# Weight-stationary products of a decoder layer: three matmuls of 256 columns in place of one of 512 and one of 256

## The chip, the cores and the metric

The kernel runs on one core of a Trainium2 chip. The metric is the device time of one execution in microseconds (us); before the change it is 1414.1 us, the median of three runs (1414.02 to 1414.1 us). All times below come from these runs or from one profiled execution of the same kernel.

## The reference

One decoder layer on 256 tokens of width 2048, batch 1, all in float32. Three sublayers follow each other, each as `h = layer_norm(2**0.25 * h + f(h))`:

```
h = x @ w_in                      # 2048 x 7216; q_a, k_a, v_a, q_b, six K/V groups, gates
y_a = sliding-window attention (16 heads, 2 K/V heads, sinks)
y_b = native sparse attention  (compressed + selected + window branches, 16 heads)
mix = (sigmoid(g_a) * (y_a @ w_branch_swa) + sigmoid(g_b) * (y_b @ w_branch_nsa)) @ w_mix_out
xa  = cross-attention of h with mem (256 rows), 4 heads of 128:  w_q, w_kv, w_o
ff  = square(relu(h @ mlp_w1)) @ mlp_w2      # 2048 x 8192 and 8192 x 2048
```

Nearly all of the work is matrix products of 256 rows with weights read once from HBM (268 MB).

## The kernel before

*High and low parts.* Every float32 operand of a large product is split in two: `h`, the value rounded to the narrower format that TensorE multiplies (`float32r`), and `l`, what is left. A product is then three: h·h, h·l and l·h. ScalarE writes `h` (line 198), VectorE subtracts it to get `l` (line 199).

*Chunks.* All weights of the layer go through one stream of chunks, mostly of 128 x 1024 numbers (512 KB), in the list `chunks`. `run_chunks` goes through the list. For a chunk it issues loads into one of five `raw` buffers, splits chunks ahead (up to three further than the chunk that TensorE works on, `AHEAD`), lets other jobs (attention, norms, transposes; the class `Side`) issue one step each, issues the chunk's matmuls, and after a block's last chunk empties the sums (`post`). A chunk index in `evac_first` has its sums emptied ahead of the last split. Nothing reorders the instructions later: each engine runs them as they were issued.

*Three kinds of products.* In `block_x` the inputs are stationary and the weights move, 512 columns at a time (lines 231 to 238). In `block_b` and `block_w` a 128 x 128 tile of weights is stationary and the inputs of all 256 rows move, so that the result comes out transposed. I call a tile with one slice of 128 rows of the weights, a k, a unit.

- `block_b` (lines 318, 319): the high weights meet the high and the low inputs, which lie side by side, in one matmul of 512 columns; the low weights meet the high inputs in one of 256. Each tile takes a whole PSUM bank, and the two halves of a bank are added afterwards by `halves` (ScalarE copies one, VectorE adds the other; lines 332 to 336). It does the four query blocks, the K and Q of the cross-attention and 14 blocks of 512 columns of the first MLP product.
- `block_w` with `mm_w` (lines 246 to 249): three matmuls of 256 columns into the same half of a bank, so that two tiles share one bank and the sums are complete. It does the first 1,024 columns of the MLP. Block c, the keys and values of the first projection, calls `mm_w` too, on other places of its chunk.

*Places of the weights.* A chunk's `shift` says where in its `h` and `l` buffers the split starts. Without a shift, h starts at byte 448 and l at byte 192 modulo 512, as in block c and `block_x`; `block_b` rotates through three shifts (h at 448, 320, 128; l at 192, 64, 384); `block_w` shifts by 16 and 112 numbers (h at 0, l at 128). The high and low inputs start at 448 throughout.

*Norms.* `norm_a` scales a piece on ScalarE (line 1037), multiplies by the gain on VectorE (1038) and adds the bias on GpSimd (1039) unless told otherwise. `finish` runs the last norm beside the last rows of the second MLP product.

The functions that are touched stand here with their lines:

Of the kernel before, what the change touches and what calls it, by code (L numbers as in the profile page):

```python
# [18 lines left out]
P = 128  # L19
# [19 lines left out]
def fp(ap):  # L39
    return ap.bitcast(F32)  # L40


class Chunk:
    def __init__(self, loads, n, mm, pre=None, with_split=None, post=None, cap=AHEAD, extra=None, parts=None, shift=(0, 0)):
        self.loads, self.n, self.mm = loads, n, mm
        self.pre, self.with_split, self.post, self.cap = pre, with_split, post, cap
        self.extra, self.shift = extra, shift
        self.parts = parts or [((lambda r: r[:, :n]),) * 2]


class Parts:
# [11 lines left out]

    def both(self, k):
        return self.tiles[k // 8][:, k % 8].rearrange("p i s -> p (i s)")
# [45 lines left out]
def layer(ctx: ExitStack, tc: tile.TileContext, x, mem, w_in, attn_sinks, rel_bias_table,  # L111
# [77 lines left out]
    def emit_splits(upto):  # L189
        while state["split"] <= min(upto, len(chunks) - 1):  # L190
# [15 lines left out]
    def run_chunks():  # L206
        for i, ch in enumerate(chunks):
# [4 lines left out]
            ahead = i + min(ch.cap, 1 if i < 3 else 2 if i < 6 else AHEAD)  # L212
# [92 lines left out]

    def block_b(w, n0, rhs, evac, tags=("acc",) * 4, pre=None):


        box = {}
        for k0 in range(0, KD, 2):  # L310
            def mm(h, l, k0=k0):
                if k0 == 0:
                    box["t"] = [bank(tag, "acc") for tag in tags]
                for a in range(2):
                    k = k0 + a
                    for t, o in enumerate(box["t"]):
                        c = slice((4 * a + t) * P, (4 * a + t + 1) * P)
                        nc.tensor.matmul(o, lhsT=h[:, c], rhs=rhs.both(k), start=k == 0, stop=False)  # L318
                        nc.tensor.matmul(o[:, :S], lhsT=l[:, c], rhs=rhs(k)[0], start=False, stop=k == KD - 1)  # L319

            def post():
                evac(box["t"])

            loads = [(lambda r: r[:, :1024].rearrange("p (a n) -> p a n", a=2),
                      w[k0 * P:(k0 + 2) * P, n0:n0 + 512].rearrange("(a p) n -> p a n", p=P))]
            chunks.append(Chunk(loads, 1024, mm, pre=pre if k0 == 0 else None, post=post if k0 + 2 == KD else None,
                                shift=((0, 96, 48)[len(chunks) % 3],) * 2))

    def halves(dst, t, scale=None):

        if scale is None:
            nc.scalar.copy(dst, t[:, S:])
            nc.vector.tensor_add(dst, t[:, :S], dst)
        else:
            nc.scalar.mul(dst, t[:, S:], scale)
            nc.vector.scalar_tensor_tensor(dst, t[:, :S], scale, dst, op0=OP.mult, op1=OP.add)
# [161 lines left out]

    def kv_parts(k):
        def pairs(v0, v1):  # L500
            return (lambda r: r[:, 128:896].rearrange("p (b v n) -> p v b n", v=2, n=P)[:, v0:v1],
                    lambda r: r[:, 128:896].rearrange("p (v b n) -> p v b n", v=2, n=P)[:, v0:v1])

        def cols(c0, c1):
            return (lambda r: r[:, c0:c1],) * 2
        if k == 0:
            return [pairs(1, 2), cols(896, 1072), pairs(0, 1), cols(0, 128)]
        return [pairs(0, 2), cols(896, 1072), cols(0, 128)]
# [62 lines left out]
    def make_c():  # L571
        for k in range(KD):
            def mm(h, l, k=k):
# [5 lines left out]
                first, last, V = k == 0, k == KD - 1, slice(640, 1072)  # L579
# [9 lines left out]
                else:  # L589
                    mm_x({(0, 0): a[0][:, :432], (1, 0): a[1][:, :432]},  # L590
                         lambda s: xh[:, rows[s]], lambda s: xl[:, rows[s]], h, l, [(640, 1072)], False, last)
# [770 lines left out]
```

## Time and profile before

| | |
|---|---|
| median of three runs | 1414.1 us |
| profiled execution | 1414.3 us, span 1412.3 us |
| TensorE matmuls | 1394.8 us busy, 99% of the span, 7,458 instructions |
| VectorE | 919.2 us, 65% |
| ScalarE | 721.7 us, 51% |
| GpSimd | 113.5 us, 8% |
| granted clock of TensorE | 0.997 of full speed on the mean |
| DMA | 190 GB/s on the mean |

Matmuls are pipelined: a row's duration runs from start to modelled end, and the next matmul starts before that end. How fast TensorE goes is read from the starts. An idle stretch of another engine is no loss while TensorE has work.

### The profile page before, as it was taken

How to read it: one execution, taken by the hardware profiler on the slowest of the kernel's cores; microseconds unless marked ns; L12 is line 12 of the kernel's file. 1: busy time of each engine (PE TensorE's matmuls, PEld its weight loads, DVE VectorE, ACT ScalarE, POOL GpSimd, SP SyncE). 2: the span in 40 equal slices, each digit the busy share in tenths (PEclk: the TensorE clock that was granted, in tenths of full speed). 3: DMA queues.
4: the chain of work that ended last, by engine and by line, in shares of the span. 5: the costliest groups of instructions: out<-in, count | busy, mean ns of one | idle time of the engine just before them, and what ended most of it. 6: DMA issues, size and time to landing. Idle time of an engine off the chain costs nothing.

```text
span 1412.3 us, 20010 instructions
## 1 busy us (share of the span) xinstructions
PE 1394.8 (99%) x7458; PEld 1196.6 (85%) x7458; DVE 919.2 (65%) x1501; ACT 721.7 (51%) x1177; POOL 113.5 (8%) x111
## 2 busy tenths in 40 slices
PE   9999999999999999999999999999999999999996
PEld 8988888888888888898898888888888888888885
DVE  5677887677764756766955656556565555755566
ACT  5566676665664444455454444444454444444452
POOL 1000221111110400220320000000000000000002
PEclk9999999999999999999999999999999999999998
DMA  8786655555557585574466666666676666576662
GB/s 267 230 258 181 186 168 164 165 153 161 149 150 252 175 297 184 174 243 139 139 186 194 186 189 190 184 190 180 194 240 195 195 193 193 179 208 193 194 193 89
DMA packets 108529, 268.43 MB, mean 190 GB/s; under 512 B 9920, under 2 KB 24832, under 8 KB 107664
## 3 DMA queue, kind: packets, MB, share of 16 engines
q1 hardware_dynamic: 106096, 256.49, 59.9%
q0 software_dynamic: 2048, 10.54, 2.2%
q8 instruction: 58, 0.95, 0.3%
q14 instruction: 39, 0.32, 0.1%
q10 hardware_dynamic: 288, 0.13, 0.1%
HBM read 264.97 MB, written 2.15 MB: 189 GB/s over the span
## 4 chain that ended last, share of the span: by engine, by line
PE 67%; issue 26%; DVE 5%; ACT 1%; POOL 0%; DMA 0%; DVEq 0%; SPq 0%; ACTq 0%; POOLq 0%
PE acc L238 22%; PE acc L318 20%; PE acc L319 10%; DVE l L199 2%; PE acc L248 1%; PE acc L249 1%; PE acc L246 1%; PE acc L231 1%; PE acc L233 1%; PE acc L232 1%; PE pt L749 1%; PE o L758 1%; PE lg L715 1%; PE lg L714 1%; PE hid L610 1%
## 5 line engine op out<-in xcount | busy, mean ns | idle before, releaser
L199 DVE TENSOR_TENSOR l<-raw,h 128x1024 fp32r<-128x1024 f32 (+4 forms) x501 | 585.9, 1178 | 381.6 <-ACT h L198 377.6
L198 ACT CAST h<-raw 128x1024 fp32r<-128x1024 f32 (+4 forms) x501 | 493.4, 994 | 441.6 <-PE acc L238 205.7
L318 PE MATMUL acc<-h2t,h 128*128 128x512 f32 x896 | 314.7, 395 | 0.0
L319 PE MATMUL acc<-h2t,l 128*128 128x256 f32 x896 | 251.7, 281 | 0.0
L318 PEld LDWEIGHTS acc<-h2t,h 128*128 128x128 f32 x896 | 168.4, 188 | 40.0
L319 PEld LDWEIGHTS acc<-h2t,l 128*128 128x128 f32 x896 | 168.6, 188 | 0.0
L238 PE MATMUL acc<-h,xt 128*128 128x512 f32 (+1 forms) x504 | 149.8, 394 | 0.0
L238 PE MATMUL acc<-l,ah 128*128 128x512 f32 x476 | 146.6, 389 | 0.0
L238 PE MATMUL acc<-h,ah 128*128 128x512 f32 x476 | 146.5, 389 | 0.0
L238 PE MATMUL acc<-h,al 128*128 128x512 f32 x476 | 146.5, 389 | 0.0
L238 PEld LDWEIGHTS acc<-l,ah 128*128 128x128 f32 x476 | 89.3, 188 | 18.6
L238 PEld LDWEIGHTS acc<-h,al 128*128 128x128 f32 x476 | 89.3, 188 | 18.6
L238 PEld LDWEIGHTS acc<-h,ah 128*128 128x128 f32 x476 | 89.3, 188 | 18.5
L238 PEld LDWEIGHTS acc<-h,xt 128*128 128x128 f32 x504 | 91.1, 188 | 14.8
L318 PE MATMUL acc<-xt,h 128*128 128x512 f32 x256 | 91.4, 397 | 0.0
L238 PE MATMUL acc<-l,xt 128*128 128x512 f32 (+1 forms) x252 | 79.6, 388 | 0.0
L319 PE MATMUL acc<-xt,l 128*128 128x256 f32 x256 | 71.9, 281 | 0.0
L238 PE MATMUL acc<-h,mt 128*128 128x512 f32 x224 | 63.2, 394 | 0.0
L745 POOL TENSOR_TENSOR p<-p,st 128x512 f32<-128x512 f32 x36 | 39.1, 1086 | 297.5 <-DVE st L740 135.2
L734 ACT ACTIVATE p<-p,st 128x256 f32<-128x256 f32 (+1 forms) x96 | 42.7, 447 | 36.4 <-DVE st L729 36.4
L318 PEld LDWEIGHTS acc<-xt,h 128*128 128x128 f32 x256 | 48.1, 188 | 10.9 <-ACT gt L550 0.3
L238 PE MATMUL acc<-h,yt 128*128 128x512 f32 x192 | 55.5, 395 | 0.0
(298 smaller groups left out, 2025.7 us busy)
## 6 DMA issues: line engine op xcount, KB each, us to landing
raw<-in_mlp_w_dram SPq DMA_DIRECT2D x256, 512.0 KB, 4.5
raw<-in_w_in_dram SPq DMA_DIRECT2D x96, 512.0 KB, 3.6
raw<-in_w_mix_out_dram SPq DMA_DIRECT2D x32, 512.0 KB, 4.7
raw<-in_w_branch_swa_dram SPq DMA_DIRECT2D x16, 512.0 KB, 3.7
raw<-in_w_branch_nsa_dram SPq DMA_DIRECT2D x16, 512.0 KB, 4.6
raw<-in_xa_w_kv_dram SPq DMA_DIRECT2D x16, 512.0 KB, 4.3
raw<-in_w_in_dram SPq DMA_DIRECT2D x16, 408.0 KB, 4.7
tbias<-udram POOLq DMA_DIRECT2D x8, 512.0 KB, 5.2
```

What stands on the lines that cost most here:

```text
L198: nc.scalar.copy(dst(h), src(raws[c]))
L199: nc.vector.tensor_sub(dst(l), src(raws[c]), fp(dst(h)))
L231: nc.tensor.matmul(a, lhsT=xh(s), rhs=h[:, c0:c1], start=first, stop=False)
L232: nc.tensor.matmul(a, lhsT=xh(s), rhs=l[:, c0:c1], start=False, stop=False)
L233: nc.tensor.matmul(a, lhsT=xl(s), rhs=h[:, c0:c1], start=False, stop=last)
L238: nc.tensor.matmul(acc[s, b], lhsT=lhs(s), rhs=rhs[:, c0:c1], start=False, stop=False)
L246: nc.tensor.matmul(a, lhsT=h[:, c], rhs=xh, start=first and (t % 2 == 0 if opens is None else t in opens), stop=False)
L248: nc.tensor.matmul(a, lhsT=h[:, c], rhs=xl, start=False, stop=False)
L318: nc.tensor.matmul(o, lhsT=h[:, c], rhs=rhs.both(k), start=k == 0, stop=False)
L319: nc.tensor.matmul(o[:, :S], lhsT=l[:, c], rhs=rhs(k)[0], start=False, stop=k == KD - 1)
L734: nc.scalar.activation(p[:, c:c + w], p[:, c:c + w], AF.Exp, bias=nm[:, i:i + 1], accum_out=sm[:, i:i + 1])
L745: nc.gpsimd.tensor_mul(pr, pr, sm.unsqueeze(2).to_broadcast([P, nr, 512 // nr]))
```

## The change

Every product with stationary weights becomes a `block_w`: `block_b` and `halves` are removed. 896 units of the MLP, 256 of the query blocks and 128 of the cross-attention change from a pair of matmuls to three. A bank then holds two complete tiles, which one copy (`copy_any`, ScalarE and VectorE in turn) empties; in the MLP ScalarE takes the relu of a bank and VectorE multiplies it by the bank itself. The MLP has eight blocks of 1,024 columns, alternately on the four `acc` banks and on the four others.

Block c's split is written in five pieces instead of three, so that its key weights begin at other places (h at 256, l at 128 modulo 512). The first two chunks of the cross-attention's K are split into two buffers of their own (`kspare`), and `boost` lets four chunks around there split one or two further ahead. `norm_a` adds the bias on VectorE now; one piece of the second norm stays on GpSimd. The last query block, in place of the first and third, has its sums emptied first.

```diff
-            for src, dst in ch.parts:
-                nc.scalar.copy(dst(h), src(raws[c]))
-                nc.vector.tensor_sub(dst(l), src(raws[c]), fp(dst(h)))
+            for src, dst, *low in ch.parts:
+                h_ap = dst(h)
+                nc.scalar.copy(h_ap, src(raws[c]))
+                nc.vector.tensor_sub((low or [dst])[0](l), src(raws[c]), fp(h_ap))
...
-            ahead = i + min(ch.cap, 1 if i < 3 else 2 if i < 6 else AHEAD)
+            ahead = i + ch.boost + min(ch.cap, 1 if i < 3 else 2 if i < 6 else AHEAD)
...
+    KEYS = (464, 496)
...
+        vals = [(lambda r: raw(r, 1, 2, 1), at(0, 2, True)), (lambda r: r[:, 896:1072], at(256, 176))]
+        ks = [(lambda r: r[:, 0:128], *keys(0, 128)), (lambda r: raw(r, 0, 3, 0), *keys(128, 3, True)),
+              (lambda r: raw(r, 0, 1, 1), *keys(512, 1, True))]
+        return vals + ks
...
-                mm_w(outs, xh, xl, h, l, first, last, (0, 1, 4), (2, 3, 4), (0, 128, 512, 256, 384))
+                mm_w(outs, xh, xl, h[:, KEYS[0]:], l[:, KEYS[1]:], first, last, (0, 1, 4), (2, 3, 4), (0, 128, 512, 256, 384))
...
-            halves(qraw[i][:, 4 * j + b, :], t)
+            copy_any(qraw[i][:, 4 * j + 2 * b:4 * j + 2 * b + 2, :], two(t))
...
-    block_b(w_in, COL_QA, xk, lambda tiles: evac_q(0, 0, tiles), tags=("lg", "pt", "acc", "acc"))
-    evac_first.add(len(chunks) - 1)
-    block_b(w_in, COL_QA + 512, xk, evac_qa)
+    block_w(w_in, COL_QA, 512, xk, lambda tiles: evac_q(0, 0, tiles), tags=("lg", "pt"))
+    block_w(w_in, COL_QA + 512, 512, xk, evac_qa)
...
-        (add or nc.gpsimd).tensor_add(v, v, gb[:, 1, c0:c0 + w])
+        (add or nc.vector).tensor_add(v, v, gb[:, 1, c0:c0 + w])
...
+    def kspare(j):
+        if j == 0:
+            box["kspare"] = box["pb"].tile([P, 4, 1024], F32R, tag="memraw", name="kspare")
+        return box["kspare"][:, 2 * j], box["kspare"][:, 2 * j + 1]
+
+    c0 = len(chunks)
+    block_w(xa_w_kv[0], 0, 512, me, evac_t("kt", None))
+    for j in range(2):
+        chunks[c0 + j].extra = lambda j=j: kspare(j)
+    for i, b in enumerate((1, 2, 2, 1)):
+        chunks[c0 - 2 + i].boost = b
...
-    block_b(xa_w_q[0], 0, hk, evac_t("qt", 128 ** -0.5), pre=lambda: side.require("ln1"))
+    block_w(xa_w_q[0], 0, 512, hk, evac_t("qt", 128 ** -0.5), pre=lambda: side.require("ln1"))
...
-                nc.gpsimd.tensor_mul(box["a"][k // KD][:, k % KD:k % KD + 2, :], two(r), two(r))
+                nc.vector.tensor_mul(box["a"][k // KD][:, k % KD:k % KD + 2, :], two(t), two(r))
...
-    block_w(mlp_w1[0], 0, 1024, hk, evac_a(0))
-    for f in range(2, 16):
-        block_b(mlp_w1[0], 512 * f, hk, evac_b(f), tags=("acc",) * 4 if f % 2 else alt)
+    for f in range(8):
+        block_w(mlp_w1[0], 1024 * f, 1024, hk, evac_a(f), tags=alt if f % 2 else ("acc",) * 4)
```

How the order of the instructions moves, at three places. On TensorE, in the first MLP product, the order before is pairs of a 512-column and a 256-column matmul (`h2t` are the transposed inputs, `h` and `l` the weights, `acc` the sums):

```order
L318 MATMUL acc<-h2t_6736,h 128x512
L319 MATMUL acc<-h2t_6736,l 128x256
L318 MATMUL acc<-h2t_6736,h 128x512
L319 MATMUL acc<-h2t_6736,l 128x256
L318 MATMUL acc<-h2t_6736,h 128x512
L319 MATMUL acc<-h2t_6736,l 128x256
```

and after the change it is threes of 256 columns at the same place:

```order
L245 MATMUL acc<-h2t_7130,h 128x256
L247 MATMUL acc<-h2t_7130,h 128x256
L248 MATMUL acc<-h2t_7130,l 128x256
L245 MATMUL acc<-h2t_7130,h 128x256
L247 MATMUL acc<-h2t_7130,h 128x256
L248 MATMUL acc<-h2t_7130,l 128x256
```

So a unit has one instruction more and the same 768 columns, and the low inputs meet the high weights in a matmul of their own.

On VectorE, where the mixer's last sums are emptied and the norm before the cross-attention begins, the order before has three splits of the K weights ahead of the sums (the last 3 of the 17; lines 1014 and 1020 are sums and statistics, 1038 the gain, `l` the low part of a split):

```order
L199 TENSOR_TENSOR l<-raw,h 128x1024 x17
L1014 SCALAR_TENSOR_TENSOR res<-res,acc 128x512 x4
L1020 BN_STATS stats<-res 128x6 x4
...
L1031 SCALAR_TENSOR_TENSOR rstd<-mv,rstd 128x1 x2
L1038 TENSOR_TENSOR res<-res,gb_5450 128x512
L199 TENSOR_TENSOR l<-raw,h 128x1024
L1038 TENSOR_TENSOR res<-res,gb_5450 128x512
L199 TENSOR_TENSOR l<-raw,h 128x1024 x3
```

and after the change five, two of them in `kspare`, with each gain (1011) followed by its bias (1012):

```order
L198 TENSOR_TENSOR l<-raw,h 128x1024 x14
L198 TENSOR_TENSOR kspare<-raw,kspare 128x1024 x2
L198 TENSOR_TENSOR l<-raw,h 128x1024 x3
L987 SCALAR_TENSOR_TENSOR res<-res,acc 128x512 x4
L993 BN_STATS stats<-res 128x6 x4
...
L1004 SCALAR_TENSOR_TENSOR rstd<-mv,rstd 128x1 x2
L1011 TENSOR_TENSOR res<-res,gb_5736 128x512
L1012 TENSOR_TENSOR res<-res,gb_5736 128x512
L198 TENSOR_TENSOR l<-raw,h 128x1024
```

Two splits moved ahead of the sums, and the bias came from GpSimd's queue into VectorE's.

On VectorE at the end of the kernel, the order before, from the first gain of the last norm to the sum of the last bank, is:

```order
L1038 TENSOR_TENSOR res<-res,gb_10109 128x512 x2
L1014 SCALAR_TENSOR_TENSOR res<-res,acc 128x512
L1020 BN_STATS stats<-res 128x6
L1038 TENSOR_TENSOR res<-res,gb_10109 128x512 x2
L1014 SCALAR_TENSOR_TENSOR res<-res,acc 128x512
```

and after the change:

```order
L1011 TENSOR_TENSOR res<-res,gb_11232 128x512
L1012 TENSOR_TENSOR res<-res,gb_11232 128x512
L1011 TENSOR_TENSOR res<-res,gb_11232 128x512
L1012 TENSOR_TENSOR res<-res,gb_11232 128x512
L987 SCALAR_TENSOR_TENSOR res<-res,acc 128x512
L993 BN_STATS stats<-res 128x6
L1011 TENSOR_TENSOR res<-res,gb_11232 128x512
L1012 TENSOR_TENSOR res<-res,gb_11232 128x512
L1011 TENSOR_TENSOR res<-res,gb_11232 128x512
L1012 TENSOR_TENSOR res<-res,gb_11232 128x512
L987 SCALAR_TENSOR_TENSOR res<-res,acc 128x512
```

Four additions that stood in GpSimd's queue stand ahead of the last sum on VectorE.

## Rows read from the trace of the kernel before

**Rows 1.** The page: busy us, share of the span, instructions.

```profile
PE 1394.8 (99%) x7458; PEld 1196.6 (85%) x7458; DVE 919.2 (65%) x1501; ACT 721.7 (51%) x1177; POOL 113.5 (8%) x111
```

**Rows 2.** Waits of TensorE: total us, times, longest; first and last of six.

```profile
PE acc L319 <- DVE l L199: 1.0, 1, 1.0
...
PE ntr L1055 <- POOL res L1039: 0.9, 1, 0.9
PE ntr L1055 <- DVE res L1048: 0.2, 1, 0.2
```

**Rows 3.** Line 318: ns min/median/max, first and last start us.

```profile
L318 PE MATMUL acc<-h2t,h x896: 387/396/403, 736.9 to 1051.1; 128*128 128x512 f32 x180
```

**Rows 4.** Timeline of TensorE in the MLP's block_b: start us, duration us.

```profile
760.04 0.40 PE L318 MATMUL acc<-h2t,h 128*128 128x512 f32 x1
760.27 0.28 PE L319 MATMUL acc<-h2t,l 128*128 128x256 f32 x1
760.39 0.40 PE L318 MATMUL acc<-h2t,h 128*128 128x512 f32 x1
```

**Rows 5.** Line 246 from 712.4 us on, second half of the block_w.

```profile
L246 PE MATMUL acc<-h2t,h x72: 276/276/369, 712.3 to 736.5; 128*128 128x256 f32 x72
```

**Rows 6.** Timeline of TensorE in the same block_w, one unit.

```profile
730.05 0.28 PE L246 MATMUL acc<-h2t,h 128*128 128x256 f32 x1
...
730.39 0.28 PE L246 MATMUL acc<-h2t,h 128*128 128x256 f32 x1
```

**Rows 7.** Timeline of TensorE in block c, 15 key matmuls, then the next.

```profile
50.46 0.28 PE L246 MATMUL acc<-xt,h 128*128 128x256 f32 x1
...
52.25 0.36 PE L238 MATMUL acc<-h,xt 128*128 128x432 f32 x1
```

**Rows 8.** Windows: length, PE, PEld, DVE, ACT, POOL busy us, clock, DMA, GB/s.

```profile
8.00:56.00 48.00, 48.00 (x346) 46.57 (x345) 28.82 (x57) 23.79 (x54) 2.21 (x3) 1.00 0.92 284
580.00:602.10 22.10, 21.10 (x124) 18.36 (x123) 20.34 (x29) 12.02 (x15) 9.29 (x7) 1.00 0.48 149
737.00:1051.70 314.70, 314.63 (x1793) 274.29 (x1791) 177.91 (x220) 137.94 (x171) 4.56 (x6) 1.00 0.65 193
```

**Rows 9.** Groups of VectorE: the addition of `halves` in the MLP, busy us, mean ns.

```profile
L333 DVE TENSOR_TENSOR sum<-acc,sum 128x256 f32<-128x256 f32 x56 | 23.4, 419 | 0.0
```

**Rows 10.** Timeline of TensorE where the second MLP product begins.

```profile
1051.35 0.28 PE L319 MATMUL acc<-h2t,l 128*128 128x256 f32 x1
1051.77 0.50 PE L231 MATMUL acc<-h,ah 128*128 128x512 f32 x1
1052.11 0.39 PE L232 MATMUL acc<-l,ah 128*128 128x512 f32 x1
```

**Rows 11.** Timeline of VectorE in the norm before the cross-attention.

```profile
587.56 2.21 DVE L199 TENSOR_TENSOR l<-raw,h 128x1024 fp32r<-128x1024 f32 x1 [0.25 <-ACT h L198]
589.70 0.68 DVE L1038 TENSOR_TENSOR res<-res,gb 128x512 f32<-128x512 f32 x1
590.30 1.21 DVE L199 TENSOR_TENSOR l<-raw,h 128x1024 fp32r<-128x1024 f32 x1
```

**Rows 12.** Timeline of GpSimd in the same norm.

```profile
590.46 2.21 POOL L1039 TENSOR_TENSOR res<-res,gb 128x512 f32<-128x512 f32 x1 [1.76 <-DVE res L1038]
```

**Rows 13.** Timeline of TensorE: four transposes of the second norm, then the next matmul.

```profile
705.50 0.60 PE L1055 MATMUL ntr<-ident,res 128*128 128x128 f32 x4
705.85 0.37 PE L246 MATMUL acc<-h2t,h 128*128 128x256 f32 x1
```

**Rows 14.** Timeline of VectorE at the end of the kernel.

```profile
1396.07 1.40 DVE L1038 TENSOR_TENSOR res<-res,gb 128x512 f32<-128x512 f32 x2 [0.89 <-ACT res L1037]
...
1398.71 2.32 DVE L1038 TENSOR_TENSOR res<-res,gb 128x512 f32<-128x512 f32 x2
1400.95 0.67 DVE L1014 SCALAR_TENSOR_TENSOR res<-res,acc 128x512 f32<-128x512 f32 x1
...
1402.76 3.15 DVE L1044 SCALAR_TENSOR_TENSOR res<-res,mv,gb 128x512 f32<-128x512 f32 x4
```

More of the change, by code (lines that the diff above doesn't have):

```diff
@@ L62, in __call__ @@
         return t[:, 0, :], t[:, 1, :]
-    def both(self, k):
-        return self.tiles[k // 8][:, k % 8].rearrange("p i s -> p (i s)")
 class Side:
@@ L304, in block_x @@
                                 extra=extra[k0 - kt + rows_last] if 0 <= k0 - kt + rows_last < len(extra) else None))
[L306 to L336, printed above, removed]
     def block_w(w, n0, n, rhs, evac, tags=("acc",) * 4, pre=None):
@@ L497, in kv_loads, with raw, at, ap @@
         return own + more
+    KEYS = (464, 496)
     def kv_parts(k):
[L500 to L508, printed above, removed]
+        def raw(r, b0, n, v):
+            return r[:, 128:896].rearrange("p (b v n) -> p b v n", v=2, n=P)[:, b0:b0 + n, v]
+        def at(c0, n, b=None):
+            def ap(t):
+                return t[:, c0:c0 + n * P].rearrange("p (b n) -> p b n", n=P) if b else t[:, c0:c0 + n]
+            return ap
+        def keys(c0, n, b=None):
+            return tuple(at(k0 + c0, n, b) for k0 in KEYS)
+        vals = [(lambda r: raw(r, 1, 2, 1), at(0, 2, True)), (lambda r: r[:, 896:1072], at(256, 176))]
+        ks = [(lambda r: r[:, 0:128], *keys(0, 128)), (lambda r: raw(r, 0, 3, 0), *keys(128, 3, True)),
+              (lambda r: raw(r, 0, 1, 1), *keys(512, 1, True))]
+        return vals + ks
     cbox = {}
@@ L578, in mm @@
                 xh, xl = xk(k)
-                first, last, V = k == 0, k == KD - 1, slice(640, 1072)
+                first, last, V = k == 0, k == KD - 1, slice(0, 432)
                 rows = [slice(s * P, (s + 1) * P) for s in range(2)]
@@ L894, in layer @@
     evac_first.add(len(chunks) - 1)
-    block_b(w_in, COL_QA, xk, lambda tiles: evac_q(0, 0, tiles), tags=("lg", "pt", "acc", "acc"))
-    evac_first.add(len(chunks) - 1)
-    block_b(w_in, COL_QA + 512, xk, evac_qa)
+    block_w(w_in, COL_QA, 512, xk, lambda tiles: evac_q(0, 0, tiles), tags=("lg", "pt"))
+    block_w(w_in, COL_QA + 512, 512, xk, evac_qa)
     for i, ch in enumerate(make_cmp()):
         chunks.insert(KD + CMP_AT + 1 + 2 * i, ch)
-    block_b(w_in, COL_QB, xk, lambda tiles: evac_q(1, 0, tiles), pre=lambda: side.require("stacks"))
+    block_w(w_in, COL_QB, 512, xk, lambda tiles: evac_q(1, 0, tiles), pre=lambda: side.require("stacks"))
+    block_w(w_in, COL_QB + 512, 512, xk, evac_qb)
     evac_first.add(len(chunks) - 1)
-    block_b(w_in, COL_QB + 512, xk, evac_qb)
     def merged():
@@ L1118, in evac @@
             for b, t in enumerate(tiles):
-                halves(box[name][:, b, :], t, scale)
+                copy_any(box[name][:, 2 * b:2 * b + 2, :], two(t), scale)
             if name == "qt":
@@ L1165, in xa_job @@
         hilo(box["oth"][:, h, :], box["otl"][:, h, :], o[:, :S])
-    block_b(xa_w_kv[0], 0, me, evac_t("kt", None))
-    evac_first.add(len(chunks) - 1)
+    def kspare(j):
[8 more added lines that the diff above has]
+        chunks[c0 - 2 + i].boost = b
     block_x(xa_w_kv[0], KD, 512, 256, me, evac_v(0))
-    block_b(xa_w_q[0], 0, hk, evac_t("qt", 128 ** -0.5), pre=lambda: side.require("ln1"))
+    block_w(xa_w_q[0], 0, 512, hk, evac_t("qt", 128 ** -0.5), pre=lambda: side.require("ln1"))
     block_x(xa_w_kv[0], KD, 768, 256, me, evac_v(256))
@@ L1194, in after_wo @@
         norm_late(1, 256, 256)
-        norm_a(0, 256, 256, add=nc.vector)
+        norm_a(0, 256, 256)
         norm_shift(1)
@@ L1212, in between_wo @@
             norm_shift(0)
-            norm_a(0, 0, 256, mul=nc.gpsimd)
+            norm_a(0, 0, 256, add=nc.gpsimd, mul=nc.gpsimd)
     def mlp_tiles(f):
```

11 lines of the change are left out of this document (2 added, 9 removed).

## The prediction

> **What bounds the kernel now.** I read the busy times first, then TensorE's waits, then the starts of its matmuls. TensorE is busy for 99% of the span [rows 1], and what it waits for comes to 5.0 us in six single waits of at most 1.0 us [rows 2]. So nearly all of the time is the distance from one matmul's start to the next, and a duration in a row is not that distance: a matmul of 256 columns is shown as 0.28 us long while the next starts 0.11 or 0.12 us later [rows 4, 6]. I therefore price the change by starts alone.
>
> In the first MLP product `block_b` takes one weight tile and one k with a matmul of 512 columns (high weights on high and low inputs side by side) and one of 256 (low weights on high inputs). I call this a unit. 896 units start between 736.9 and 1051.1 us [rows 3]: 314.2 / 895 = 0.3511 us for one. The starts show how it is made up: 0.23 to 0.24 us for the 512 columns, 0.12 us for the 256 [rows 4].
>
> The same trace holds the form that the change puts in its place. The first 1,024 columns of the MLP go through `block_w`, whose unit is three matmuls of 256 columns with the weights where the change puts them all. 72 units of its second half, where no transposes stand between them, start between 712.3 and 736.5 us [rows 5]: 24.2 / 71 = 0.3409 us, and inside a chunk the starts are 0.11 to 0.12 us apart, 0.34 us for a unit [rows 6]. A third row is the warning: the key products of block c are also triples of 256 columns, with high weights at byte 448 and low at 192 modulo 512, and 15 matmuls take from 50.46 to 52.25 us, 0.1193 us each and 0.358 us a unit [rows 7]. Three short matmuls are thus cheaper than the pair only in one of the two placements that the trace shows; the break-even is 0.3511 / 3 = 0.117 us a matmul.
>
> **The change part by part.** The sum is made against the profiled execution, 1414.3 us (span 1412.3 us and 2.0 us around it); the median of the three runs is 0.2 us lower.
>
> *Units.* 896 of the MLP, 256 of the four query blocks and 128 of the cross-attention's K and Q move from `block_b` to `block_w`: 1,280. At 0.3511 - 0.3409 = 0.0102 us each this is 13.1 us less. The bounds are 0.340 us a unit [rows 6], 14.2 us less, and 0.343 us if jobs between the chunks disturb the short matmuls more than the long ones, 10.4 us less. In 16 of the units the weights come from two borrowed buffers at byte 448; at the price of rows 7 they give back 16 x 0.017 = 0.3 us.
>
> *Block c.* The 80 key units keep their three matmuls and get other places: low at 128, high at 256 modulo 512. No row has this pair. It lies between no gain (0.358 us stays) and the price of rows 5, 80 x 0.017 = 1.4 us. The low half is that of the good rows and the high half that of neither, so I take the middle, 0.7 us less. The five splits in place of three add two instructions each to ScalarE and VectorE per chunk; between 8 and 56 us VectorE is busy for 28.8 of 48 us [rows 8], and about 0.3 us more in each of 16 chunks fits there. Without that cover each late split would cost its own 0.3 us.
>
> *MLP evacuation.* Per two tiles of 256 columns VectorE loses two adds out of the banks and two products, 0.42 us each as the add shows [rows 9], and gets one product of 512 columns, at most as long as two of 256. It is busy for 177.9 of 314.7 us in this stage [rows 8], and the blocks go alternately to two sets of four banks, so nothing waits for it: zero. At the end of the stage there is something: the second MLP product begins on the banks that the last `block_b` has just filled, and its first two matmuls start 0.42 and 0.34 us after the ones before them [rows 10], against 0.12 and 0.23 us elsewhere. With eight blocks the last one has the other set. That is 0.3 us, and 0.11 us for each of four banks: 0.7 us less.
>
> *Start of the cross-attention.* TensorE waits 1.0 us for a low split there [rows 2]. The split that it waits for takes VectorE 2.21 us, where the next one takes 1.21 us [rows 11], beside an addition on GpSimd; such an addition takes up to 2.2 us there [rows 12]. In the new order five chunks of K weights are split before the sums of the mixer are emptied, where three were, so TensorE has 5 x 8 x 0.341 = 13.6 us of work while the norm begins. The wait goes, with the slower starts around it: 1.3 us less (bounds 0.5 and 1.5).
>
> *Additions of the norms.* 18 additions of 512 columns go from GpSimd to VectorE. In the second norm TensorE waits 0.9 us for GpSimd and 0.2 us for VectorE [rows 2]; an addition of about 0.7 us directly behind its product ends sooner than one of 2.1 us on another engine. 1.0 us less (bounds 0.3 and 1.2). What is late next is VectorE itself: in each chunk of both norms it then has a product and an addition (1.4 us), a split (1.2 us) and a low part out of a bank (0.7 us, as the products) [rows 11], 3.3 us in all, beside a chunk and four transposes on TensorE, 2.7 + 0.4 = 3.1 us [rows 13]. With the chunks split ahead this is covered; the price without that is a rival below.
>
> *The end.* Here the additions cost. Before, VectorE runs two products (1396.07 us), the sum and statistics of one bank, two products, and the last bank's sum at 1400.95 us, just after the last matmul has ended, with the additions beside it on GpSimd [rows 14]. In the new order each product has its addition behind it on VectorE. From 1396.07 us on: ten operations of 0.7 us (four products, four additions, one sum, one statistics) end at 1403.1 us, 2.0 us later than before. Without GpSimd the four products after it need 2.8 us rather than 3.15 us [rows 14]: 0.3 us back. 1.7 us more (bounds 1.4 and 2.3).
>
> Sum: -13.1 + 0.3 - 0.7 - 0.7 - 1.3 - 1.0 + 1.7 = -14.8 us. From the median this gives 1399.3 us. All the good bounds together give 17.3 us less (1396.8 us), all the poor ones 9.3 us less (1404.8 us).
>
> **A rule that speaks against it.** The rows say that a 512-column matmul inside `block_b` costs 0.23 to 0.24 us and a 256-column one in `block_w` 0.113 us. The Trainium skill, "TensorE: Matmul & The Clock Gate", section "Back-to-back issue gap", gives an isolated matmul N / 2.4 + 2.5 ns at the full clock, a fixed price for each. By that rule, as an estimate, the pair takes 215.8 + 109.2 = 325.0 ns and the three 327.5 ns, and 1,280 units cost 3.2 us more. This trace disagrees: the pair takes 351 ns and the three 341 ns.
>
> **Rivals.**
> 1. *VectorE becomes the bound in the norms.* 3.3 us against 3.1 us a chunk, and the first norm starts with 2.4 + 2.4 us of sums and statistics. If the chunks split ahead are used up, eight chunks in each of two norms lose 0.2 us, 3.2 us, and the 2.3 us for waits there stay: 1399.3 + 5.5 = 1404.8 us. For it: VectorE is busy 20.3 of 22.1 us there [rows 8]. Against it: that includes its slow stretches of 2.2 us beside GpSimd, which go.
> 2. *The new placement gains nothing outside the block that had it.* Then a unit stays at 0.351 us and only the waits and the end are left, -1.3 us: 1412.8 us. For it: block c's triples are at 0.358 us. Against it: the rows of the good block are of the same inputs, the same kind of chunk and the same rate of loads as the 896 units.
> 3. *Slower: every matmul has its own fixed price, and the good block is a special case.* Three matmuls at the 0.1193 us of rows 7 take 0.358 us, 1,280 x 0.007 = 8.8 us more; with the other terms 1414.1 + 8.8 - 1.3 = 1421.6 us. It decides as soon as a short matmul's starts are more than 0.117 us apart in the MLP. For it: 80 units of rows 7, and the 256-column matmuls of rows 4 are 0.12 us apart too. Against it: the 72 units of rows 5. The rule above would be a weak form of this.
> 4. *The change does not do what it says.* The order shows that it does: three rows of 256 columns stand where the pairs stood, and none of the pairs is left. I give it nothing.
>
> **How the numbers follow.** The forecast has 0.85, rival 1 0.08, rival 2 0.04, rival 3 0.03. No measured difference under 0.2% (2.8 us) can be told from none. The forecast's own range is 1397 to 1403 us, and rival 1 reaches to about 1405; a range of 1396.5 to 1404 us leaves out rivals 2 and 3, most of rival 1 and the forecast's edges, about 2 in 10. Forecast and rival 1 are faster by more than 0.2%: 0.93. Rival 2 is within it: 0.04. Rival 3 is slower: 0.03.
>
> **What would show it.** In the changed profile the three matmul lines of the weight-stationary products should start 0.113 to 0.115 us apart in the MLP, and a first MLP product of 128 chunks should take about 128 x 2.73 = 349 us apart from the norm's transposes. The waits of TensorE for the low split and for GpSimd in the norms should be gone. The last bank's sum should start about 2 us later after the last matmul than before, and the end after it should be no longer. The prediction is wrong if the matmuls start more than 0.117 us apart in the MLP, if TensorE has a new wait for VectorE of more than 2 us in the norms, or if the span after the last matmul grows by more than 3 us.

## The result and the profile after

The changed kernel takes 1398.3 us (median of four runs, 1398.16 to 1398.4 us) against 1414.1 us: 0.9889 of the time, 95% interval 0.9876 to 0.9901. The forecast was 1399.3 us. The profiled execution has a span of 1396.5 us, 15.8 us less than before.

The busy line of the page (columns as in [rows 1]) shows that the bound is the same engine:

```profile
PE 1380.3 (99%) x8738; PEld 1240.8 (89%) x8738; DVE 897.3 (64%) x1452; ACT 716.1 (51%) x1162; POOL 75.9 (5%) x89
```

TensorE has 1,280 matmuls more and is busy 14.5 us less. Its waits, all of them this time (columns as in [rows 2]):

```profile
PE pt L723 <- POOL p L719: 1.0, 1, 1.0
PE warm L139 <- DVE rowmask L145: 0.9, 1, 0.9
PE o L732 <- DVE ptl L352: 0.4, 1, 0.4
PE ntr L1028 <- DVE res L1021: 0.2, 1, 0.2
```

The wait for a low split (1.0 us), the one for GpSimd in the second norm (0.9 us) and one of 1.0 us for the first high split of the kernel are gone; the 0.2 us for VectorE in the norm stayed. One wait is new: 0.4 us for VectorE (`ptl`), in the attention right behind the query blocks.

I compare the stages by the starts at which they begin on TensorE, in us from the start of each span:

| stage begins | before | after | gained in the stage before it | forecast |
|---|---|---|---|---|
| first product with `yt` (block c and the query blocks lie before) | 278.41 | 275.27 | 3.14 | 3.3 |
| K of the cross-attention | 579.99 | 576.80 | 0.05 | 0 |
| Q of the cross-attention | 618.77 | 614.05 | 1.53 | 1.65 |
| first MLP product | 688.40 | 683.09 | 0.59 | 0.65 |
| second MLP product | 1051.77 | 1035.06 | 11.40 | 10.4 |
| end of the last matmul | 1400.57 | 1383.40 | 0.46 | 0.4 |
| end of the span | 1412.3 | 1396.5 | -1.37 | -1.7 |

The forecasts are the prediction's terms put to these stages: 256 units and block c (2.6 + 0.7); the start of the cross-attention with 64 units less the borrowed buffers (1.3 + 0.65 - 0.3); 64 units; 896 units, the norm and the first slower start (9.1 + 1.0 + 0.3); the other four banks (0.4).

The 3.14 us of the first row are a sum of more parts than its forecast. The first key matmul starts 0.40 us sooner (7.24 us, where it was 7.64; it lies between 7.12 and 7.99 us in the runs below, which leave the kernel's start as it is, so this can be chance), block c gains 0.7 us and the query blocks 2.95 us. From the last of the query blocks' matmuls to the first product with `yt` it then takes 115.2 us instead of 114.3: 0.9 us are lost there, 0.4 of them in the new wait, and the prediction had nothing for them.

The windows of the same three stages as [rows 8], with the same columns:

```profile
8.00:56.00 48.00, 48.00 (x349) 46.54 (x348) 30.71 (x86) 27.41 (x84) 2.23 (x3) 1.00 0.90 288
577.00:599.00 22.00, 22.00 (x193) 22.00 (x191) 19.83 (x33) 10.99 (x15) 1.10 (x2) 1.00 0.44 137
731.00:1034.80 303.80, 303.80 (x2683) 303.80 (x2682) 154.59 (x142) 133.16 (x143) 1.14 (x2) 1.00 0.64 201
```

In the last one 2,683 matmuls stand in 303.80 us: 0.1132 us each, 0.3397 us a unit, against 0.3511 us of [rows 3] and the 0.3409 us that the prediction took from [rows 5]. VectorE falls from 177.9 us of 314.7 to 154.6 us of 303.8 there. The timeline of TensorE in this product (start, duration) has what stands in place of [rows 4]:

```profile
760.00 0.28 PE L245 MATMUL acc<-h2t,h 128*128 128x256 f32 x1
760.11 0.28 PE L247 MATMUL acc<-h2t,h 128*128 128x256 f32 x1
760.22 0.28 PE L248 MATMUL acc<-h2t,l 128*128 128x256 f32 x1
760.34 0.28 PE L245 MATMUL acc<-h2t,h 128*128 128x256 f32 x1
```

The duration is still 0.28 us, as in [rows 6]; only the starts tell the pace. The change of product, where [rows 10] had distances of 0.42 and 0.34 us, now runs through:

```profile
1034.94 0.28 PE L248 MATMUL acc<-h2t,l 128*128 128x256 f32 x1
1035.06 0.40 PE L230 MATMUL acc<-h,ah 128*128 128x512 f32 x1
1035.29 0.40 PE L231 MATMUL acc<-l,ah 128*128 128x512 f32 x1
```

Block c, 15 key matmuls and the next one, as [rows 7]:

```profile
49.51 0.28 PE L245 MATMUL acc<-xt,h 128*128 128x256 f32 x1
...
51.26 0.36 PE L237 MATMUL acc<-h,xt 128*128 128x432 f32 x1
```

1.75 / 15 = 0.1167 us each, where it was 0.1193 us. VectorE in the norm before the cross-attention, as [rows 11]:

```profile
583.45 0.69 DVE L1011 TENSOR_TENSOR res<-res,gb 128x512 f32<-128x512 f32 x1 [0.36 <-ACT res L1010]
584.18 0.69 DVE L1012 TENSOR_TENSOR res<-res,gb 128x512 f32<-128x512 f32 x1
584.79 1.22 DVE L198 TENSOR_TENSOR l<-raw,h 128x1024 fp32r<-128x1024 f32 x1
```

The addition (1012) takes 0.69 us on VectorE, where GpSimd took 2.21 us [rows 12], and the split behind it takes 1.22 us. And VectorE at the end, as [rows 14]:

```profile
1378.97 0.69 DVE L1011 TENSOR_TENSOR res<-res,gb 128x512 f32<-128x512 f32 x1 [0.88 <-ACT res L1010]
...
1385.61 0.68 DVE L987 SCALAR_TENSOR_TENSOR res<-res,acc 128x512 f32<-128x512 f32 x1
...
1387.42 2.73 DVE L1017 SCALAR_TENSOR_TENSOR res<-res,mv,gb 128x512 f32<-128x512 f32 x4
```

The last sum starts 2.2 us after the last matmul's end, where it was 0.4 us.

### The profile page after: what moved, and what is told of

Read it like the earlier page. It is cut to its first block, busy times and chain, and to the rows that moved or that the text cites. A ratio compares the mean times of both kernels' runs of the same rounds, so it can differ in the third digit from the quotient of the medians.

```text
span 1396.5 us, 22476 instructions
## 1 busy us (share of the span) xinstructions
PE 1380.3 (99%) x8738; PEld 1240.8 (89%) x8738; DVE 897.3 (64%) x1452; ACT 716.1 (51%) x1162; POOL 75.9 (5%) x89
## 4 chain that ended last, share of the span: by engine, by line
PE 95%; DVE 3%; ACT 1%; issue 0%; POOL 0%; DVEq 0%; POOLq 0%; ACTq 0%
PE acc L237 46%; PE acc L245 12%; PE acc L248 12%; PE acc L247 12%; PE acc L230 2%; PE acc L232 2%; PE acc L231 2%; PE pt L723 1%; DVE l L198 1%; PE o L732 1%; PE lg L689 1%; PE hid L584 1%; PE lg L688 1%; PE o L731 1%; PE ntr L1028 1%; PE tr L366 1%
## 5 line engine op out<-in xcount | busy, mean ns | idle before, releaser
L245 PE MATMUL acc<-h2t,h 128*128 128x256 f32 x1024 | 283.4, 277 | 0.0
L247 PE MATMUL acc<-h2t,h 128*128 128x256 f32 x1024 | 282.8, 276 | 0.1
L248 PE MATMUL acc<-h2t,l 128*128 128x256 f32 x1024 | 282.8, 276 | 0.0
L247 PEld LDWEIGHTS acc<-h2t,h 128*128 128x128 f32 x1024 | 192.3, 188 | 0.3 <-DVE h2t L352 0.3
L245 PEld LDWEIGHTS acc<-h2t,h 128*128 128x128 f32 x1024 | 192.2, 188 | 0.2 <-ACT h2t L351 0.2
L248 PEld LDWEIGHTS acc<-h2t,l 128*128 128x128 f32 x1024 | 192.2, 188 | 0.0
L245 PE MATMUL acc<-xt,h 128*128 128x256 f32 x336 | 93.7, 279 | 0.0
L248 PE MATMUL acc<-xt,l 128*128 128x256 f32 x336 | 93.2, 277 | 0.0
L247 PE MATMUL acc<-xt,h 128*128 128x256 f32 x336 | 93.1, 277 | 0.0
L245 PEld LDWEIGHTS acc<-xt,h 128*128 128x128 f32 x336 | 63.2, 188 | 0.2
L247 PEld LDWEIGHTS acc<-xt,h 128*128 128x128 f32 x336 | 63.2, 188 | 0.1
```

What stands on the lines that cost most here:

```text
L245: nc.tensor.matmul(a, lhsT=h[:, c], rhs=xh, start=first and (t % 2 == 0 if opens is None else t in opens), stop=False)
L247: nc.tensor.matmul(a, lhsT=h[:, c], rhs=xl, start=False, stop=False)
L248: nc.tensor.matmul(a, lhsT=l[:, c], rhs=xh, start=False, stop=last and (t % 2 == 1 if closes is None else t in closes))
```

## The experiments

The first question was why the short matmuls are cheaper: because three equal ones follow each other, or because of where their weights lie. One theory says place, the rival says form; a third, the prediction's slower rival, says that each matmul has a fixed price. Places are bytes modulo 512. The edits are made in the changed kernel unless another is named.

### Triples at the old places

```diff
-            chunks.append(Chunk(loads, 1024, mm, pre=pre if k0 == 0 else None, shift=(16, 112),
+            chunks.append(Chunk(loads, 1024, mm, pre=pre if k0 == 0 else None, shift=(0, 0),
```

High weights at 448, low at 192; all else as changed.

> The changed kernel with the weights of all its stationary products back at bytes 448 (high) and 192 (low) modulo 512. If the place of the weights sets the pace, a unit takes the 0.358 us of block c before, and 1,392 units at 0.017 us each make it 24 us slower than the changed kernel: about 1422 us. If three matmuls of equal length are what counts, the starts stay 0.1135 us apart and it takes about 1398 us.

1425.1 us, 1.0079 of the kernel before (1.0064 to 1.0094): slower than it. The first MLP product by line 245 (ns min/median/max, first and last start), here and below it in the changed kernel:

```profile
L245 PE MATMUL acc<-h2t,h x1024: 277/283/365, 690.1 to 1061.8; 128*128 128x256 f32 x171
```

```profile
L245 PE MATMUL acc<-h2t,h x1024: 276/276/369, 683.1 to 1034.7; 128*128 128x256 f32 x171
```

371.7 us against 351.6 us for the same 1,024 units and transposes. So 26.8 us hang on two numbers of a split's start, and every block's triples (query blocks, K, Q, MLP) go at 0.120 us. This is the price of [rows 7]: the starts are 0.120 us apart, and 0.0203 us for each of 1,392 units would be 28 us.

### High weights at 256

```diff
-            chunks.append(Chunk(loads, 1024, mm, pre=pre if k0 == 0 else None, shift=(16, 112),
+            chunks.append(Chunk(loads, 1024, mm, pre=pre if k0 == 0 else None, shift=(80, 112),
```

This is the pair of places that block c got, in the long products.

> The changed kernel with the high weights at 256 and the low ones at 128 modulo 512, as block c has them after the change. In block c the starts are then about 0.117 us apart. If that comes from the place, the MLP takes this pace too: 0.350 us a unit, 1,392 x 0.009 = 12.5 us slower than the changed kernel, about 1411 us. If it comes from the short runs of 15 matmuls between others in block c, the MLP stays at 0.1135 us and the time at about 1398 us.

1398.6 us, 0.989 (0.9873 to 0.9906), no different from the changed kernel:

```profile
L245 PE MATMUL acc<-h2t,h x1024: 276/276/369, 683.9 to 1035.5; 128*128 128x256 f32 x171
```

351.6 us again. So 256 and 128 are as good as 0 and 128, and block c's 0.1167 us is not a price of this place. What is left as the cause is that its 15 matmuls stand alone between products of another kind. No run tests that, but the changed kernel's trace fits it: in the 15 from 49.51 us on, the first ten starts are 0.118 us apart on the mean and the last four 0.113 to 0.114 us.

### Pairs at the new places

In the kernel before, in place of the three rotating shifts:

```diff
-                                shift=((0, 96, 48)[len(chunks) % 3],) * 2))
+                                shift=(16, 112)))
```

> The kernel before, with its pairs of 512 and 256 columns kept, and only their weights at 0 (high) and 128 (low) modulo 512. If the place sets the pace, the pair takes 0.227 + 0.1135 = 0.3405 us instead of 0.351 and 1,280 units save 13 to 14 us: about 1400 us, without the other parts of the change. If the form matters, the pair stays at 0.351 us and the time at 1414 us.

1416.4 us, 1.0017 (1.0007 to 1.0026). The pairs by line 318:

```profile
L318 PE MATMUL acc<-h2t,h x896: 388/397/397, 737.2 to 1053.4; 128*128 128x512 f32 x180
```

316.2 / 895 = 0.3533 us a unit, a little more than before [rows 3]. The same places are no help to the pairs: the starts are 0.233 us apart after the long matmul and 0.120 us after the short one. This looked like form and place together; the pairs at two other pairs of places, below, say more.

### The moving weights of `block_x` at other places

```diff
-                                cap=kt - 1 - k0 + len(extra) if k0 >= kt - rows_last else AHEAD,
+                                cap=kt - 1 - k0 + len(extra) if k0 >= kt - rows_last else AHEAD, shift=(112, 16),
```

The products with stationary inputs get their weights at 384 and 256 in place of 448 and 192; the inputs stay at 448.

> The changed kernel with the moving weights of the other products (block_x, 512 columns, inputs stationary at 448) at 384 (high) and 256 (low), so that the stationary operand stands 64 and 192 bytes behind the moving one, as it does in the good stationary products. If the distance between the two operands is what counts, the 0.2267 us between the starts of some 2,900 matmuls falls towards 0.220 us and the kernel gains up to 20 us: 1378 to 1390 us. If only the place of the stationary operand counts, nothing moves: 1398 us. If the old places were the good ones for this form, it is slower: above 1401 us.

1405.7 us, 0.9941 (0.9926 to 0.9956): 7.3 us slower than the changed kernel.

### The stationary inputs at 0

A tile of 16 numbers is allocated ahead of the second MLP product's inputs, which then begin at 0 in place of 448:

```diff
+    padah = []
...
+        if not padah:
+            padah.append(box["pc"].tile([P, 16], F32, tag="padah", name="padah"))
```

> The changed kernel with the inputs of the second MLP product (stationary there, the weights moving at 448 and 192) moved from byte 448 to byte 0 modulo 512. If a stationary operand at a multiple of 128 bytes beside a moving one that is not is good for matmuls of equal length whatever their size, as the three placements so far say for 256 columns, the 0.2267 us between the starts of these 1,500 matmuls falls by up to the same 0.0066 us: about 1388 us. If 512 columns hide what the place costs, or the distance decides otherwise, it stays at 1398 us.

1408.1 us, 0.9958 (0.9944 to 0.9973). The gain that was hoped for is a loss of 9.7 us. Line 237 in the second MLP product, in the changed kernel, with the weights moved, and with the inputs moved:

```profile
L237 PE MATMUL acc<-h,ah x476: 389/389/389, 1037.8 to 1365.8; 128*128 128x512 f32 x159
```

```profile
L237 PE MATMUL acc<-h,ah x476: 388/394/398, 1040.1 to 1372.9; 128*128 128x512 f32 x159
```

```profile
L237 PE MATMUL acc<-h,ah x476: 393/396/398, 1037.8 to 1375.5; 128*128 128x512 f32 x159
```

328.0, 332.8 and 337.7 us for the same work. "The stationary operand at a multiple of 128 is good" falls: what 256 columns like, 512 columns do not. With moving and stationary operand 0 apart modulo 128 the long matmuls start 0.227 us apart. With 64 apart it is 0.230 us on the mean where the weights were moved and 0.233 us where the inputs were (0.226 to 0.236 us by what follows what). The triples are the other way round, 0.120 us with 0 apart and 0.113 us with 64.

That the distance is what counts is not shown by this. No run moves both operands by the same amount, and in the triples only the weights were ever moved. One product of 256 columns did have its moving operand moved: the V of the cross-attention, in the run with the moved weights. By the distance its starts should have fallen from 0.120 to 0.113 us. Line 237 there, in the changed kernel and with the weights moved:

```profile
L237 PE MATMUL acc<-h,met x112: 278/283/469, 602.0 to 653.3; 128*128 128x256 f32 x112
```

```profile
L237 PE MATMUL acc<-h,met x112: 278/281/469, 604.3 to 655.4; 128*128 128x256 f32 x112
```

Their starts are 0.120 and 0.118 us apart (medians). So the distance alone is no rule for 256 columns.

### Places between

Both kinds of products moved by 32 bytes (and in the second run by 16: `shift=(4, 4)` and `(20, 116)`), with the end as in "GpSimd's additions at the end" below:

```diff
-                                cap=kt - 1 - k0 + len(extra) if k0 >= kt - rows_last else AHEAD,
+                                cap=kt - 1 - k0 + len(extra) if k0 >= kt - rows_last else AHEAD, shift=(8, 8),
-            chunks.append(Chunk(loads, 1024, mm, pre=pre if k0 == 0 else None, shift=(16, 112),
+            chunks.append(Chunk(loads, 1024, mm, pre=pre if k0 == 0 else None, shift=(24, 120),
```

> The changed kernel with the last norm's additions on GpSimd (1396.8 us by itself), and the weights of both kinds of products 32 bytes further: moving ones at 480 and 224, stationary ones at 32 and 160 modulo 512. So far the distance from the moving to the stationary operand explains all: at 512 columns 0 modulo 128 gives 0.2267 us and 64 gives 0.230 to 0.236; at 256 columns 64 gives 0.1134 and 0 gives 0.120. If this goes evenly between the two, both forms have a pace between theirs here, 0.230 and 0.117 us, and the time is about 1396.8 + 2,900 x 0.003 + 1,392 x 3 x 0.003 = 1418 us. If only the half of 128 bytes counts in which the distance falls, one form keeps its pace. If a better place lies between, it is below 1396 us.

> The same with 16 bytes in place of 32: moving weights at 464 and 208, stationary ones at 16 and 144. If the pace changes evenly with the distance, about half of the loss at 32 bytes: 1407 us. If pieces of 32 or 64 bytes count, the paces of 0.2267 and 0.1134 us stay and the time is 1396.8 us. If a better place lies between, it is below 1396 us.

1430.9 us, 1.012 (1.0091 to 1.015), and 1428.1 us, 1.010 (1.0071 to 1.0129). The short matmuls, first with 32, then with 16 bytes:

```profile
L245 PE MATMUL acc<-h2t,h x1024: 278/282/367, 693.5 to 1058.6; 128*128 128x256 f32 x171
```

```profile
L245 PE MATMUL acc<-h2t,h x1024: 276/280/364, 691.8 to 1056.8; 128*128 128x256 f32 x171
```

365.1 and 365.0 us, where the good place has 351.6 and the worst tried 371.7. The long matmuls of line 237 in the second MLP product start between 1061.7 and 1399.4 us and between 1059.9 and 1395.1 us: 337.7 and 335.2 us, where the good place has 328.0 and the worst tried 337.7. Both kernels are slower than even the smooth change between the places that was put at 1418 and 1407 us: sixteen bytes lose two thirds of what is to be lost with the short matmuls and three quarters with the long ones. No better place was found. Finer steps were not tried.

### Pairs at places chosen by the weights that are loaded next

While a matmul runs, the weights of the next one are loaded (PEld is busy for 1196.6 us beside TensorE's 1394.8 [rows 1]). In a triple, current and next weights have the same distance from the moving inputs modulo 128; in a pair of two places they need not. I read the pairs so: the long matmul wants the *next* (low) weights 0 apart, the short one wants the *next* (high) weights 64 apart. That is low at 192, high at 0. The complement is low at 128, high at 448. Both in the kernel before:

```diff
-                                shift=((0, 96, 48)[len(chunks) % 3],) * 2))
+                                shift=(16, 0)))
```

```diff
-                                shift=((0, 96, 48)[len(chunks) % 3],) * 2))
+                                shift=(0, 112)))
```

> The kernel before with its pairs, the high weights at 0 and the low ones at 192. The weights of the next matmul are loaded while one runs, so the 512 columns run beside the load of the low weights (distance 0 modulo 128, the good one for 512 so far) and the 256 columns beside that of the high ones (distance 64, the good one for 256). If each matmul's pace hangs on its own length and that distance alone, a pair takes 0.2267 + 0.1134 = 0.340 us and 1,280 pairs save 14 us: 1400 us. If the good places hold only in a row of equal lengths, the pair stays near 0.351 us: 1412 to 1416 us.

> The complement: pairs with the high weights at 448 and the low ones at 128, so that both matmuls have the poor distance by the rule of the run beside it. If the rule holds for pairs, 0.233 + 0.120 = 0.353 us or more: 1416 us or more, and clearly slower than the run with 0 and 192. If the places don't matter between unequal lengths, the two runs take the same time, 1412 to 1416 us.

The first takes 1404.0 us, 0.993 (0.9915 to 0.9945), the second 1409.6 us, 0.997 (0.9958 to 0.9981). Line 318 in each:

```profile
L318 PE MATMUL acc<-h2t,h x896: 389/389/390, 736.2 to 1040.5; 128*128 128x512 f32 x180
```

```profile
L318 PE MATMUL acc<-h2t,h x896: 396/396/397, 736.1 to 1046.4; 128*128 128x512 f32 x180
```

0.3400 and 0.3467 us a unit. With high at 0 and low at 192 the pair of the MLP is as fast as the triple's 0.3397 us:

```profile
759.63 0.39 PE L318 MATMUL acc<-h2t,h 128*128 128x512 f32 x1
759.85 0.28 PE L319 MATMUL acc<-h2t,l 128*128 128x256 f32 x1
759.97 0.39 PE L318 MATMUL acc<-h2t,h 128*128 128x512 f32 x1
```

One edit of a shift thus gives 9.9 us of the kernel before's time, without one more matmul. But 14 us were expected, and the 9.9 us are the MLP's 896 units alone. In the query blocks, in Q and in most of K the same places leave the pair at 0.351 us, while the triples of the changed kernel go at their good pace there too. Q (`h1t`) in the kernel before, with high at 0 and low at 192, and in the changed kernel:

```profile
L318 PE MATMUL acc<-h1t,h x64: 387/396/403, 618.8 to 640.9; 128*128 128x512 f32 x64
```

```profile
L318 PE MATMUL acc<-h1t,h x64: 393/395/396, 618.2 to 640.3; 128*128 128x512 f32 x64
```

```profile
L245 PE MATMUL acc<-h1t,h x64: 276/276/281, 614.1 to 635.5; 128*128 128x256 f32 x64
```

22.1, 22.1 and 21.4 us for 63 units: 0.351, 0.351 and 0.340 us each. In the run with 0 and 192, K (`met`) even changes its pace on the way, at TensorE's wait for a low split:

```profile
581.51 0.39 PE L318 MATMUL acc<-met,h 128*128 128x512 f32 x1
...
581.85 0.39 PE L318 MATMUL acc<-met,h 128*128 128x512 f32 x1
...
589.30 0.39 PE L319 MATMUL acc<-met,l 128*128 128x256 f32 x1 [1.28 <-DVE l L199]
589.52 0.39 PE L318 MATMUL acc<-met,h 128*128 128x512 f32 x1
...
589.87 0.39 PE L318 MATMUL acc<-met,h 128*128 128x512 f32 x1
```

A pair takes 0.34 us before that wait and 0.35 us after it, with the weights and inputs at the same places. So the places alone do not fix the pace of a pair.

The complement was expected slower than before and is not: its long matmul is as slow as foreseen (0.233 us), but its short one takes 0.113 us, not 0.120. The pairs at 0 and 128 above miss the other way: their short matmul has the next weights 64 apart and takes 0.120 us. So the rule by the next weights alone is incomplete. It gave the best pair of places that was tried; what else counts (the place of the current weights, or when the load falls within the matmul) stays open.

### Without the buffers for the K weights

`kspare` and `boost` are taken out:

```diff
-    for j in range(2):
-        chunks[c0 + j].extra = lambda j=j: kspare(j)
-    for i, b in enumerate((1, 2, 2, 1)):
-        chunks[c0 - 2 + i].boost = b
```

> The changed kernel without the two borrowed split buffers and without boost: three chunks of K weights split ahead, 8.2 us of work for TensorE. If it was these that took the wait for the low split away, it comes back with 1 to 2 us, since VectorE now has sums, statistics, two gains and two biases (about 9 us) ahead of the next split: 1399.5 to 1400.5 us. If the wait had come only from GpSimd's additions beside the split, which are gone, no wait returns: 1398.3 us.

1399.0 us, 0.9894 (0.9877 to 0.991); the end is as in the changed kernel. The wait of [rows 2] is back:

```profile
PE acc L248 <- DVE l L198: 0.7, 1, 0.7
```

From the start of K to that of Q it takes 37.92 us instead of 37.25. That is the size of the median's difference, 0.7 us; single runs of the two kernels lie 0.3 us apart and the intervals overlap, so it is the wait and not the median that shows the cause.

### The biases on GpSimd again

```diff
-        (add or nc.vector).tensor_add(v, v, gb[:, 1, c0:c0 + w])
+        (add or nc.gpsimd).tensor_add(v, v, gb[:, 1, c0:c0 + w])
...
-        norm_a(0, 256, 256)
+        norm_a(0, 256, 256, add=nc.vector)
```

> The changed kernel with the biases of all norms on GpSimd again, as before. If my terms hold, TensorE waits about 0.9 us for GpSimd in the second norm again (1.0 us slower) and the end after the last matmul falls from 13.1 to 11.7 us (1.4 us faster): about 1398 us in all, no difference that can be told. If the additions on VectorE are what saved the start of the cross-attention, a wait for a low split is there too: 1399 to 1400 us.

1398.7 us, 0.9892 (0.9877 to 0.9907): no difference, because two terms cancel. TensorE has the wait of [rows 2] back:

```profile
PE ntr L1028 <- POOL res L1012: 0.9, 1, 0.9
```

while the stretch after the last matmul takes 12.1 us in place of 13.1 (11.7 was expected). From the start of K to that of Q it takes 37.25 us, as in the changed kernel, and no wait for a low split is there: with the borrowed buffers, GpSimd's additions do not bring it back.

### GpSimd's additions at the end

Only the last norm's biases go back:

```diff
-                norm_a(0, c, 512)
+                norm_a(0, c, 512, add=nc.gpsimd)
```

> The changed kernel with only the last norm's four additions on GpSimd. If they are what lengthened the end, the time after the last matmul falls from 13.1 to 11.7 us and the whole to about 1397 us. If something else in the end got longer, it stays at 13.1 us and 1398.3 us.

1396.8 us, 0.9879 (0.9864 to 0.9894), the fastest of all that ran, 1.5 us below the changed kernel's median. The interval overlaps with that kernel's (they ran on different chips), but their traces differ where the edit is. VectorE at the end:

```profile
1381.42 2.31 DVE L1011 TENSOR_TENSOR res<-res,gb 128x512 f32<-128x512 f32 x2
1383.66 0.67 DVE L987 SCALAR_TENSOR_TENSOR res<-res,acc 128x512 f32<-128x512 f32 x1
...
1385.46 3.15 DVE L1017 SCALAR_TENSOR_TENSOR res<-res,mv,gb 128x512 f32<-128x512 f32 x4
```

The last sum starts 0.45 us after the last matmul's end (1383.21 us), and what follows that end takes 11.7 us, as before the change. The products beside GpSimd are slower (2.31 us for two, where the changed kernel needs 1.4), and still it is the shorter way.

## Why the prediction was right

- *Units.* Right, and a little better than put, in all blocks: 0.3397 us a unit in the MLP, not 0.3409 us. The 24.2 us of [rows 5] run over 72 units with some longer matmuls among them (369 ns at most); [rows 6] had 0.34 us. 896 x (0.3511 - 0.3397) = 10.2 us, with the norm's 0.9 and the second product's 0.3 us, is the 11.4 us of that stage. The MLP product lasts 352 us with the norm's transposes; 349 us without them was forecast.
- *Form or place.* The prediction put the gain down to triples "only in one of the two placements". The runs bear that out and add to it. At the old places triples make the kernel slower than before, so the form alone gains nothing. Pairs with high at 0 and low at 192 are as fast as triples in the MLP, so for those 896 units the place alone would do. In the other 384 units only the triples got the good pace; there it took form and place together. Why a pair has two paces at the same places is open.
- *Block c.* 0.7 us was forecast; 240 x (0.1193 - 0.1167) = 0.6 us. The size was right by luck, since it was the middle between two bounds, and the reason was wrong: not the place at 256, which is as good as 0 in a long product.
- *Borrowed buffers.* Right: their 16 units at 448 start within 5.4 us, 0.36 us each, as [rows 7] said:

```profile
L245 PE MATMUL acc<-met,kspare x16: 278/283/283, 576.8 to 582.2; 128*128 128x256 f32 x16
```

- *Start of the cross-attention.* The wait and the split of 2.21 us [rows 11] are gone. Of the forecast 1.3 us for the two, the buffers hold 0.7; the stage as a whole gained 1.53 us of 1.65.
- *What the sum left out.* The 0.4 us at the kernel's start and the 0.9 us lost behind the query blocks stand in no term. They partly cancel, and with the units' better pace the first stage comes to 3.14 us of 3.3: nearer than its terms.
- *Norms.* The 0.9 us are shown by the biases' return. VectorE did not become the bound: it is busy 19.8 of 22 us at the start of K, and TensorE does not wait for it. The first rival is out.
- *Second MLP product's start.* Both slower starts are gone; 0.46 us in that stage and 0.3 us at its border stand for the 0.7 us.
- *The end.* 1.37 us instead of 1.7. From the first gain to the last sum it is 6.64 us (1378.97 to 1385.61) where it was 4.88: 1.76 us, not 2.0 (and the prediction's own 1403.1 us lie 2.1 us, not 2.0, behind the 1400.95 us of [rows 14]). The four products after it take 2.73 us for 3.15: 0.42 us, not 0.3.
- *The other rivals.* No gain outside the good block: excluded by the 896 units. The fixed price for each matmul: in the MLP three of 256 columns cost 0.3397 us and the best pair 0.3400, so a third instruction costs nothing here. The rule that the prediction quoted from the Trainium skill, "TensorE: Matmul & The Clock Gate", section "Back-to-back issue gap", makes the triple 2.5 ns dearer than the pair; measured at their best places it is 0.3 ns cheaper. The slower world that this rival foresaw (1421.6 us) does exist: it is the triple at the old places, with 1425.1 us.

## What to carry to other kernels

When TensorE is busy throughout, compare the distance between starts in every block of the same kernel: where two blocks do the same work at two paces, look at the byte at which each operand begins, before the form is changed. Try the operands at both distances (0 and 64 modulo 128 in this kernel) and for each length of matmul apart, since what one length wants slowed the other here. Then read the pace in every block: at one and the same places the pairs were fast in the MLP and not in the query blocks, while three equal matmuls kept their pace in all of them. Work that moves to a faster engine should be looked at once more at the kernel's end, where it may stand ahead of the last sum.

## What the runs showed of the hardware

The pace of float32r matmuls with a weight load for each depends on where the operands begin in a partition: 0.113 or 0.120 us for triples of 256 columns, and for the 512 columns of the second MLP product 0.227 us or, on the mean, 0.230 to 0.233 us. The granted clock is at full speed in either case (1.00 in the MLP of the changed kernel and of the one with the old places). Between triples at good and at bad places that is 26.8 us of 1398. In pairs of 512 and 256 columns the place is not all: 0.340 and 0.351 us were seen at the same places.

The Trainium skill, "TensorE: Matmul & The Clock Gate", section "Step-by-step: what each phase is for", says that TensorE reads the moving operand and the next weights through two independent ports, so that a weight load takes no read bandwidth from the running matmul. It names no dependence on where the operands begin; these runs show one, since each edit moved only that and the pace changed. That the load and the read of the moving operand meet in the same part of the memory is my reading; no run here shows it.

Beside GpSimd's additions VectorE is slower: two products of 512 columns take 2.31 us where they take 1.4 us without, and a split 2.21 us [rows 11] where it takes 1.22 us. The Trainium skill, "SBUF — State Buffer", section "Who interferes with whom", says that a VectorE operation with two inputs in this memory and a GpSimd operation share a pair of ports, which one of them locks for its whole length. The traces agree that they interfere. The loss for two products (0.9 us) is smaller than one of the additions beside them (1.4 to 1.5 us), but the addition that was running had only 1.2 us left when they began (1381.42 to 1382.59 us), so this is no evidence against such a lock.
